# Starting every larger SBUF tile behind the first stage at a multiple of 128 bytes

## The chip, the cores and the metric

One core of one Trainium2 chip runs the whole kernel as one program. The metric is device time in microseconds (us): the median of three runs of the kernel before is 3519.21 us (3517.99 to 3523.26). One further execution was taken by the hardware profiler; all rows below are from it.

## The reference

Two transformer blocks of two layers each, on 1024 tokens of width 1024, in fp32. Cut to what matters here:

```
first_block, layers i = 0, 1:
    mix = diff_attention(h)  (i = 0)  or  pool_mixer(h)  (i = 1)
    h   = layer_norm(ALPHA * h + mix)          # mix ends in a 1024x1024 projection
    ffn = hier_moe(h)                          # 32 experts, 2 of them for each token
    h   = layer_norm(ALPHA * h + ffn)
hier_moe, for one expert:  y = (silu(x @ w_gate) * (x @ w_up)) @ w_down     # 1024 -> 512 -> 1024
second_block, layers l = 0, 1:
    h = rms_norm(x) * (1 + scale) + shift;  proj = h @ w_in
    x = x + gate * (concat(retention, mla, gla) @ w_out)
```

The result must have fp32 accuracy, so a product x @ w is computed as three products of rounded parts: high*high, high*low, low*high.

## The kernel before, in words

**Products.** `split` (L80, L81) makes the two fp32r parts of an operand: ScalarE writes the rounded copy, VectorE subtracts it from the original. `mm3` (L84 to L87) issues the three matmuls of one block of 128 rows. In `matmul(out, w, x)` the second argument is held in the array (stationary, 128x128, loaded by LDWEIGHTS), the third streams through it (moving, here mostly 512 columns).

**First stage** (0 to 303 us): `phase_qkv`, in the pools `pk0`, `v`, `p1` and `p1w`. Moving `xh`/`xl` or `wh`, stationary `whi`/`wlo` or `xh`/`xl`.

**Attention** (303 to 505 us): pools `p2k`, `p2c`, `p2p`; `oT` on the right side of SBUF.

**proj_ln** (twice, from 505 and from about 1390 us): for each of 8 tiles of 128 tokens, 16 `mm3` with stationary `ah`/`al` (parts of the activations; `first` for tile 0 of layer 0) and moving weights `wcut`, L87 and before; then layer norm and the router. Its pool is `pl`. In layer 1 two of the four weight pieces are in the pool `wo` on the right side, the other two in the pool `H`; a tile's 8 blocks of k use one piece of each for either half of the columns.

**Moe.run** (twice, from about 653 and from about 1540 us): for each of 32 experts 48 matmuls into `gu` (stationary `xgh`/`xgl`, the gathered tokens) and 24 into `accy` (stationary `hh`/`hl`), moving always `wcut`, plus 12 transposes. PE's order, ScalarE's and VectorE's are fixed by `in_order`. Each of the six pieces of weights of an expert (1 MB) is loaded by SyncE into a raw buffer `wraw` (nine of them in turn), split into one of four `wcut` buffers, and used by 12 matmuls. `gather` reads the tokens and `result` scatters the output by indirect DMA on GpSimd.

**Pooling.run** (1250 to 1390 us): stationary weights `wcut`, moving activations `x2` (the name `pool` in the trace): 64 `mm3` with 256 columns, then 96 with 512 columns; then the group products on `ph`.

**Second** (2110 us to the end): both layers of the second block, in `t4`, `rg`, `wr`, `mla`, `mle`, `ox`, `om`, `H`, `R` and others.

**Where tiles start.** Without a request the allocator rounds each tile's bytes per partition up to a multiple of 32 and puts one behind the other. A small tile therefore shifts all that come after it in its pool, and the pools stacked upon that one. Start addresses of the program before, as remainders of a division by 128 (first kernel stage, `H`, `R` and nearly all of `Second`: remainder 0):

| tile | role in the matmuls | remainder by 128 |
|---|---|---|
| `xgh`, `xgl`, `hh`, `hl` (MoE) | stationary | 64 |
| `ah`, `al` (proj_ln) | stationary | 64 |
| `x2` of Pooling (`pool` in the trace) | moving, 512 or 256 columns | 96 |
| `wcut` in the pool `wo` (proj_ln, layer 1) | moving, 512 columns | 96 |
| `wcut` in `H`, `first`, `xh`, `xl`, `whi`, `wlo`, `ph`, `mx` | stationary or moving | 0 |
| `p`, `pT`, `oraw`, `cmb`, `idb` (attention) | stationary or moving, 128 columns | 32 or 96 |
| `hT` (router) | stationary, 36 columns moving | 32 in layer 0, 0 in layer 1 |
| `wraw`, nine in turn in the MoE | not in a matmul | 0 (six), 96 (three) |

All tiles of remainder 0 that are used with 512 moving columns start 384 bytes beyond a multiple of 512. In the MoE the shift comes from the router's pool `rt`, below: its tiles `wr`, `br`, `lg`, `OH` and on take 15296 bytes, which is 64 more than a multiple of 128.

Of the kernel before, what the change touches and what calls it, by code (L numbers as in the profile page):

```python
# [17 lines left out]
PSUM = bass.MemoryType.PSUM  # L18
# [9 lines left out]
def host_consts():  # L28
    c = {}
    f = np.float32  # L30
    c["ident"] = np.eye(P, dtype=f)
    inv = (500000.0 ** (-np.arange(0, 16, 2) / 16)).astype(f)
    ang = (np.arange(S, dtype=f)[:, None] * inv[None, :]).astype(f)
    co, si = np.cos(ang).astype(f), np.sin(ang).astype(f)
    cT = np.tile(co.T, (8, 1))
    sT = np.concatenate([np.tile(si.T, (4, 1)), np.tile(-si.T, (4, 1))], 0)
    c["rope1"] = np.ascontiguousarray(np.stack([cT, sT], 1))
    i = np.arange(P)
    c["cmask"] = np.where(i[None, :] > i[:, None], f(-2.0 ** 100), f(0)).astype(f)
    c["iota"] = np.tile(np.arange(P, dtype=f)[None], (P, 1))  # L40

    kt = np.arange(2)[:, None, None] * np.array([0, S]) + np.arange(NT)[None, :, None] * P
    c["tcode"] = (kt[None] + i[:, None, None, None] - 2 * S).astype(f)
    c["tri"] = (i[:, None] < i[None, :]).astype(f)

    c["mavg"] = np.tile((1.0 / np.minimum(np.arange(1, 17)[None, :], np.array([2, 4, 8, 16])[:, None]))[None], (P, 1, 1)).astype(f)

    ch = i // 64
    lg = np.log1p(-np.exp2(-5.0 - np.arange(4)))
    vis = (ch[:, None] <= ch[None, :]).astype(np.float64)  # L50
    dm = np.exp(lg[None, :, None] * np.abs(i[:, None] - i[None, :])[:, None, :]) * vis[:, None, :] / 8.0
    c["r_dm"] = dm.astype(f)
    c["r_kw"] = (np.exp((127.0 - i)[:, None] * lg[None, :]) / 8.0).astype(f)
    hd = 2 * np.arange(2)[None, :] + ch[:, None]
    c["r_qw"] = np.exp((i + 1.0)[None, None, :] * lg[hd][:, :, None]).astype(f)
    c["r_sd"] = np.exp(128.0 * lg[hd]).astype(f)

    inv32 = (10000.0 ** (-np.arange(32) / 32)).astype(f)
    inv16 = (10000.0 ** (-np.arange(16) / 16)).astype(f)
    c["inv"] = np.stack([np.tile(inv32, 4), np.tile(inv16, 8)], 1).astype(f)  # L60
    c["rsgn"] = np.stack([np.tile(np.repeat([1.0, -1.0], 32), 2), np.tile(np.repeat([-1.0, 1.0], 16), 4)], 1).astype(f)
    c["bones"] = (ch[:, None] == ch[None, :]).astype(f)
    c["tri16"] = ((i[:, None] <= i[None, :]) & (ch[:, None] == ch[None, :])).astype(f) / f(16)
    same = ch[:, None] == ch[None, :]
    c["gmask"] = np.stack([(i[None, :] >= i[:, None]) & same, (i[None, :] < i[:, None]) & same], 1).astype(f)
    c["qmask"] = np.where(ch[None, :] > ch[:, None], f(-2.0 ** 100), f(0)).astype(f)
    return c


class Ctx:  # L70
    def __init__(self, tc, a):
        self.tc, self.nc, self.a = tc, tc.nc, a
        self.n = 0
# [192 lines left out]
class Attention:  # L266
# [50 lines left out]
    def tile(self):  # L317
        return self.PS.tile([P, S], F32, tag="S", name=self.g.name("S"), bufs=3)
# [1594 lines left out]
def b2_consts(g, pool, tmp):  # L1913
    nc, a = g.nc, g.a
    def load(name, shape):
# [21 lines left out]


CONST = host_consts()
INPUTS = ["x", "attn_w_qkv", "attn_w_o", "attn_lq1", "attn_lk1", "attn_lq2", "attn_lk2", "attn_sub_g", "pool_w_in",  # L1940
          "pool_w_grp", "pool_scale", "pool_w_out", "ln_g", "ln_b", "moe_w_grp_router", "moe_b_grp_router",
# [3 lines left out]


def program(tc, a, out):
    nc = tc.nc
    g = Ctx(tc, a)
    dram = lambda name, shape: nc.dram_tensor(name, shape, F32).ap()  # L1950
# [11 lines left out]
    with pool_of("const") as cp, ExitStack() as r2:  # L1962
# [106 lines left out]
        with ExitStack() as cb:  # L2069
            pool = cb.enter_context(L.pool("cb1", 3))  # L2070
# [51 lines left out]
```

## Time and profile before

| what | us |
|---|---|
| median of the three runs | 3519.21 |
| the profiled execution, its own time | 3515.97 |
| its span, first to last instruction | 3514.2 |
| TensorE busy in the span (PE) | 3299.4 |
| VectorE busy (DVE) | 2407.2 |
| ScalarE busy (ACT) | 1825.6 |

The profiled execution's time is 1.8 us above its span and 3.2 us below the median of the runs. A busy TensorE need not be one at its best rate: the end of a matmul is modelled, and matmuls overlap in the records (one lasts 388 to 394 ns, the next begins some 227 ns after it began). So its rate is read from the starts of consecutive matmuls, which a timeline gives to 10 ns, over long runs without a gap.

### The profile page before, as it was taken

What the parts mean: (1) busy time and instruction counts of PE and PEld (TensorE: products, weight loads), DVE (VectorE), ACT (ScalarE), POOL (GpSimd) and SP (SyncE); (2) the same over time, 40 slices, a digit from 0 to 9 for tenths busy, and PEclk for the clock granted to TensorE, in tenths of its full rate; (3) what the DMA queues carried; (4) which work ended last, traced back from release to release, by engine and by line L of the source; (5) the groups of instructions that cost most, each with busy time, mean ns of one, the idle gap of its engine ahead of it and who ended that gap; (6) DMA issues with size and microseconds to landing.
All of it is one profiled execution on the core that took longest, in us unless ns stands there. A gap on an engine that the chain in (4) does not pass through costs nothing. (4 is left out here: it accounts for less than half of the span.)

```text
span 3514.2 us, 44298 instructions
## 1 busy us (share of the span) xinstructions
PE 3299.4 (94%) x16904; PEld 2730.2 (78%) x16904; DVE 2407.2 (69%) x2850; ACT 1825.6 (52%) x2601; POOL 829.2 (24%) x627
## 2 busy tenths in 40 slices
PE   8999999999999969999999993999999899998988
PEld 7888878888888857888888882877777788676776
DVE  5665888799999975679999996532366443425653
ACT  3224872588878733248778772122467212244751
POOL 1121221133333231113333326321002122400120
PEclk9999999999999989999999996999999999999999
DMA  8666524699999832179999984211322632023144
GB/s 260 216 188 173 146 87 162 248 389 381 380 379 378 303 128 77 75 265 381 388 387 382 376 314 170 37 31 38 116 73 91 203 91 43 19 81 108 61 138 156
DMA packets 302967, 695.86 MB, mean 198 GB/s; under 512 B 57518, under 2 KB 154576, under 8 KB 286300
## 3 DMA queue, kind: packets, MB, share of 16 engines
q1 hardware_dynamic: 263964, 634.11, 51.8%
q0 software_dynamic: 36480, 50.45, 4.3%
q10 hardware_dynamic: 2304, 8.39, 0.6%
q8 instruction: 136, 2.23, 0.3%
q14 instruction: 83, 0.68, 0.1%
HBM read 625.59 MB, written 98.66 MB: 206 GB/s over the span
## 5 line engine op out<-in xcount | busy, mean ns | idle before, releaser
L81 DVE TENSOR_TENSOR wcut<-wraw,wcut 128x2048 fp32r<-128x2048 f32 (+1 forms) x401 | 902.7, 2267 | 66.7 <-ACT wcut L80 66.7
L80 ACT ACTIVATE wcut<-wraw 128x2048 fp32r<-128x2048 f32 (+1 forms) x401 | 754.0, 1900 | 124.8 <-PE accy L87 98.1
L85 PE MATMUL gu<-wcut,xgh 128*128 128x512 f32 x1024 | 408.7, 399 | 0.4 <-ACT xgh L80 0.4
L87 PE MATMUL gu<-wcut,xgl 128*128 128x512 f32 x1024 | 403.8, 394 | 0.0
L86 PE MATMUL gu<-wcut,xgh 128*128 128x512 f32 x1024 | 401.3, 392 | 0.0
L806 POOL DMA_INDIRECT yd<-yo,idx x64 | 171.4, 2679 | 799.8 <-DVE yo L805 780.2
L85 PE MATMUL A<-h,whi 128*128 128x512 f32 (+1 forms) x736 | 287.3, 391 | 6.2 <-ACT h L80 3.3
L87 PE MATMUL A<-h,wlo 128*128 128x512 f32 (+1 forms) x736 | 281.8, 383 | 3.8 <-DVE wlo L81 3.8
L86 PE MATMUL A<-h,whi 128*128 128x512 f32 (+1 forms) x736 | 282.8, 384 | 0.9 <-DVE h L81 0.9
L80 ACT ACTIVATE whi<-wraw 128x1024 fp32r<-128x1024 f32 (+2 forms) x86 | 70.9, 856 | 310.7 <-PE A L86 251.4
L85 PEld LDWEIGHTS gu<-wcut,xgh 128*128 128x128 f32 x1024 | 193.9, 189 | 38.4 <-ACT xgh L80 0.8
L86 PEld LDWEIGHTS gu<-wcut,xgh 128*128 128x128 f32 x1024 | 192.8, 188 | 39.3
L87 PEld LDWEIGHTS gu<-wcut,xgl 128*128 128x128 f32 x1024 | 192.4, 188 | 39.7 <-DVE xgl L81 0.9
L81 DVE TENSOR_TENSOR wlo<-wraw,whi 128x1024 fp32r<-128x1024 f32 (+2 forms) x86 | 83.1, 973 | 200.8 <-ACT whi L80 200.5
L87 PE MATMUL accy<-wcut,hl 128*128 128x512 f32 x512 | 201.9, 394 | 0.3 <-DVE hl L81 0.3
L86 PE MATMUL accy<-wcut,hh 128*128 128x512 f32 x512 | 200.6, 392 | 0.0
L85 PE MATMUL accy<-wcut,hh 128*128 128x512 f32 x512 | 199.1, 389 | 1.6 <-ACT hh L80 1.6
L746 POOL DMA_INDIRECT xg<-hd,idx x64 | 182.7, 2854 | 49.3 <-DVE idx L736 30.4
L85 PEld LDWEIGHTS A<-h,whi 128*128 128x128 f32 x736 | 144.8, 197 | 34.6 <-ACT h L80 4.5
L87 PEld LDWEIGHTS A<-h,wlo 128*128 128x128 f32 x736 | 143.8, 195 | 31.5 <-DVE wlo L81 4.7
L86 PEld LDWEIGHTS A<-h,whi 128*128 128x128 f32 x736 | 144.5, 196 | 27.6 <-issue 3.1
L1708 POOL TENSOR_TENSOR z<-z,lo 128x1024 f32<-128x1024 f32 x8 | 19.0, 2375 | 471.4 <-DMA lo<-rrd 235.8
(518 smaller groups left out, 7835.9 us busy)
## 6 DMA issues: line engine op xcount, KB each, us to landing
wraw<-in_moe_w_gate SPq DMA_DIRECT2D x128, 1024.0 KB
wraw<-in_moe_w_up SPq DMA_DIRECT2D x128, 1024.0 KB
wraw<-in_moe_w_down SPq DMA_DIRECT2D x128, 1024.0 KB
spare<-in_ada_w SPq DMA_DIRECT2D x48, 512.0 KB
wraw<-in_w_in SPq DMA_DIRECT2D x40, 512.0 KB
y<-yd SPq DMA_DIRECT2D x16, 1024.0 KB
wraw<-in_attn_w_qkv SPq DMA_DIRECT2D x12, 1024.0 KB
mx<-mixd SPq DMA_DIRECT2D x24, 512.0 KB
```

The lines of the kernel that those rows point to most:

```text
L80: self.nc.scalar.activation(hi, src, AF.Copy)
L81: (lo_eng or self.nc.vector).tensor_tensor(lo, src, hi.bitcast(F32), op=ALU.subtract)
L85: mm(out, wh, xh, start=start, stop=False)
L86: mm(out, wh, xl, start=False, stop=False)
L87: mm(out, wl, xh, start=False, stop=stop)
L746: self.g.nc.gpsimd.indirect_dma_start(out=xg, out_offset=None, in_=self.hd, in_offset=bass.IndirectOffsetOnAxis(ap=idx, axis=0), bounds_ch ...
L806: st = nc.gpsimd.indirect_dma_start(out=self.yd, out_offset=bass.IndirectOffsetOnAxis(ap=yidx, axis=0), in_=y, in_offset=None, bounds_chec ...
L1708: nc.gpsimd.tensor_tensor(z, z, rb, op=ALU.mult)
```

## The change

Two wrappers are put around the tile pools. Every tile whose elements per partition number 128 or more asks for a start at a multiple of 128 bytes, in all SBUF pools but the constants (`const`, and so `const2` too), `pk0`, `v` and those of the first stage (`p1`, `p1w`). Tiles of fewer elements are as before. No instruction is added or removed.

```diff
+class AlignedPool:
+    def __init__(self, pool):
+        self.pool = pool
+    def __getattr__(self, name):
+        return getattr(self.pool, name)
+    def tile(self, shape, dtype, **kw):
+        if math.prod(shape[1:]) >= 128:
+            kw["align_bytes"] = 128
+        return self.pool.tile(shape, dtype, **kw)
+
+class Aligned:
+    def __init__(self, tc):
+        self.tc = tc
+    def __getattr__(self, name):
+        return getattr(self.tc, name)
+    @contextmanager
+    def tile_pool(self, **kw):
+        with self.tc.tile_pool(**kw) as pool:
+            yield pool if kw.get("space") is PSUM or kw["name"].startswith(("const", "pk0", "v", "p1")) else AlignedPool(pool)
...
 def program(tc, a, out):
+    tc = Aligned(tc)
     nc = tc.nc
     g = Ctx(tc, a)
```

## Rows read from the trace of the kernel before

**Rows 1.** The page: TensorE's busy time, share and instructions

```profile
PE 3299.4 (94%) x16904; PEld 2730.2 (78%) x16904; DVE 2407.2 (69%) x2850; ACT 1825.6 (52%) x2601; POOL 829.2 (24%) x627
```

**Rows 2.** Busy time by stretch: proj_ln, MoE, Pooling, proj_ln, MoE; header names the columns

```profile
core 0: us, PE busy (x) PEld busy (x) DVE busy (x) ACT busy (x) POOL busy (x), PEclk, DMA share, GB/s
528.00:612.00 84.00, 84.00 (x444) 70.87 (x443) 70.69 (x185) 25.01 (x40) 11.35 (x10) 1.00 0.43 157
660.00:1130.00 470.00, 469.62 (x2204) 392.00 (x2203) 446.48 (x314) 377.43 (x316) 147.94 (x50) 1.00 0.99 378
1300.00:1350.00 50.00, 50.00 (x216) 40.32 (x216) 36.95 (x45) 13.03 (x17) 16.57 (x17) 1.00 0.07 22
1400.00:1500.00 100.00, 98.75 (x520) 82.90 (x519) 59.48 (x119) 18.95 (x29) 13.95 (x11) 1.00 0.24 91
1560.00:2060.00 500.00, 500.00 (x2347) 417.67 (x2346) 478.00 (x335) 400.91 (x337) 162.96 (x56) 1.00 1.00 381
```

**Rows 3.** Waits, 700 to 1100 us: total us, times, longest; releaser behind the arrow

```profile
ACT wcut L80 <- PE accy L87: 37.6, 46, 0.8
DVE wcut L81 <- ACT wcut L80: 17.7, 22, 0.8
```

**Rows 4.** Waits of SyncE's queue, which issues the loads, 700 to 1100 us

```profile
SPq L121 <- DVE wcut L81: 343.1, 135, 3.3
```

**Rows 5.** Busy time in two gapless runs of matmuls: first stage, then MoE

```profile
92.75:112.24 19.49, 19.49 (x87) 16.14 (x86) 13.31 (x21) 3.05 (x5) 0.57 (x1) 1.00 0.50 162
909.43:922.47 13.04, 13.04 (x58) 10.71 (x57) 12.23 (x9) 11.42 (x9) 2.37 (x1) 1.00 1.00 362
```

**Rows 6.** Timeline, proj_ln layer 0: start us, us, instruction; 9, then 33 matmuls between

```profile
526.63 0.39 PE L85 MATMUL acc<-wcut,first 128*128 128x512 f32 x1
...
528.67 0.39 PE L85 MATMUL acc<-wcut,ah 128*128 128x512 f32 x1
...
536.22 0.39 PE L85 MATMUL acc<-wcut,ah 128*128 128x512 f32 x1
```

**Rows 7.** Timeline, Pooling, 512 columns: 45 matmuls from the first to the second

```profile
1300.97 0.40 PE L85 MATMUL acc<-pool,wcut 128*128 128x512 f32 x1
...
1311.47 0.40 PE L85 MATMUL acc<-pool,wcut 128*128 128x512 f32 x1
```

**Rows 8.** Timeline, proj_ln layer 1: 9, then 11 matmuls between

```profile
1409.02 0.40 PE L85 MATMUL acc<-wcut,ah 128*128 128x512 f32 x1
...
1411.13 0.39 PE L85 MATMUL acc<-wcut,ah 128*128 128x512 f32 x1
...
1413.65 0.39 PE L87 MATMUL acc<-wcut,al 128*128 128x512 f32 x1
```

**Rows 9.** Timelines, 256 columns: first stage (33 matmuls between), Pooling (30 between)

```profile
67.92 0.28 PE L85 MATMUL acc<-whi,xh 128*128 128x256 f32 x1
...
71.89 0.28 PE L85 MATMUL acc<-whi,xh 128*128 128x256 f32 x1
...
1280.83 0.28 PE L85 MATMUL acc<-pool,wcut 128*128 128x256 f32 x1
...
1284.43 0.28 PE L85 MATMUL acc<-pool,wcut 128*128 128x256 f32 x1
```

**Rows 10.** Groups by shape: count, busy us, mean ns, idle before; first of three lines

```profile
L85 PE MATMUL gu<-wcut,xgh 128*128 128x512 f32 x1024 | 408.7, 399 | 0.4 <-ACT xgh L80 0.4
L87 PE MATMUL accy<-wcut,hl 128*128 128x512 f32 x512 | 201.9, 394 | 0.3 <-DVE hl L81 0.3
L85 PE MATMUL acc<-wcut,ah 128*128 128x512 f32 x240 | 96.7, 403 | 0.0
L85 PE MATMUL acc<-pool,wcut 128*128 128x512 f32 x96 | 38.1, 397 | 0.0
```

**Rows 11.** Tile wcut, 700 to 1100 us: duration ns min/median/max, first and last start

```profile
L80 ACT ACTIVATE wcut<-wraw x135: 1912/1918/1927, 699.9 to 1099.7; 128x2048 fp32r<-128x2048 f32 x135
L81 DVE TENSOR_TENSOR wcut<-wraw,wcut x135: 2280/2289/2295, 700.2 to 1098.7; 128x2048 fp32r<-128x2048 f32 x135
```

## The prediction

> **What bounds the kernel now.** I read the page first: TensorE is busy for 94% of the span [rows 1]. [...] Next the waits, to see who paces whom in the MoE. The reader is to see three things. No row has TensorE waiting. ScalarE waits for TensorE to give back a buffer of split weights (37.6 us in 400), and VectorE waits behind ScalarE (17.7 us) [rows 3]. And each of the 135 weight loads of that stretch waits until VectorE has emptied a raw buffer [rows 4], so the loads run behind the matmuls and not ahead of them, though the queues are busy for 0.99 of the time [rows 2]. TensorE sets the pace there, and whatever each matmul saves should come out at the end.
>
> Last I read the starts of consecutive matmuls, the one thing that an address could change. These are the pairs of rows to compare. In the first stage, with all operands at remainder 0, 87 matmuls start within 19.49 us; from first to last start (92.75 to 112.25) that is 86 steps in 19.50 us, 226.7 ns each. In the MoE, with a stationary operand at remainder 64, 57 steps take 13.05 us (909.43 to 922.48), 228.9 ns each [rows 5]. Heavier loading could make the same difference, so I looked for a place where nothing changes but the address. In proj_ln of layer 0 the stationary tile changes from `first` (0) to `ah`/`al` (64) in the middle of a run, with the moving weights in the same pool: 9 steps take 2.04 us (226.7 ns) up to that point and 33 steps take 7.55 us (228.8 ns) behind it [rows 6]. The step is there at the very matmul where the tile changes.
>
> **The change part by part.** It adds and removes no instruction; it moves tiles by 32 to 96 bytes. What can change is the rate of instructions that touch them, and the address overlaps from which the program takes its waits.
>
> Stationary tiles from 64 to 0, moving operand at 0. The MoE has (1024 + 512) x 3 = 4608 such matmuls over both layers [rows 10]. At 228.9 - 226.7 = 2.2 ns that is 10.1 us. proj_ln has 240 x 3 = 720 with `ah`/`al` [rows 10]; 192 of them, in layer 1, stream weights from the pool `wo` and are counted below. The other 528 give 528 x 2.2 = 1.2 us.
>
> Moving tiles from 96 to 0. In Pooling, 45 steps of 512 columns take 10.50 us, 233.3 ns [rows 7]; 96 x 3 = 288 matmuls [rows 10] at 233.3 - 226.7 = 6.6 ns give 1.9 us. In proj_ln of layer 1 both operands are off: 9 steps take 2.11 us (234.4 ns) with weights from `wo`, and the next 11, weights from `H`, take 2.52 us (229.1 ns) with the same stationary tile [rows 8]. From 234.4 to 226.7 ns, 192 matmuls give 1.5 us.
>
> Moves that I cost at nothing. Pooling's 192 matmuls of 256 columns have a moving operand at 96 and take 3.60 us for 30 steps, 120.0 ns; those of the first stage, all at 0, take 3.97 us for 33, 120.3 ns [rows 9]. At that width the address does not show, and I take it that it shows no more at 128 columns (attention, transposes, router), where the work per load is smaller still; if it did, as much as 2.2 ns on some 1500 such matmuls of the attention would be 3 us. On ScalarE and VectorE, the weights' splits read raw buffers at 0 and at 96 in turn, and all 135 lie between 1912 and 1927 ns and between 2280 and 2295 ns [rows 11]; I take 0 there. The DMAs into those raw buffers are hidden as long as the loads wait for buffers and not the reverse [rows 4]. If a load became late, its cover would be gone and ScalarE's split and then TensorE would stand; I bound this as a rival. Waits from overlaps: tiles move by less than 128 bytes while the tiles they may touch are 2 to 16 KB long, so I expect the same pairs to overlap; the bound is a wait or two of the length seen in the stage, 0.8 us [rows 3].
>
> The sum is 10.1 + 1.2 + 1.9 + 1.5 = 14.7 us. How much of it reaches the end? In the MoE all, by the reading above: afterwards an expert's 72 matmuls take 0.16 us less, and VectorE, with 446.48 us of 470 [rows 2], the next in line, is free for 0.9 us in each of the 26 or so experts of that stretch. In proj_ln and Pooling, 4.6 us, nearly all; I keep 0 to 4.6 for the range. The profiled execution would go from 3515.97 to 3501.3 us. Its time stood 3.2 us below the median of the runs; carried over, the median goes from 3519.2 to 3504.5 us. I say 3504.
>
> [...]
>
> **The rivals.**
>
> *No change: the starts are not what makes the difference* (5%). If every 32-byte start were alike, the steps in rows 6 and 8 would need another cause. What could be one is the second tile that `ah` and `al` are, against the single `first`; but the first stage uses two tiles as well, `whi` and `wlo`, and runs at 226.7 ns. The time would be 3519. That the change doesn't reach its tiles is part of this rival; the pools concerned are none of the names left out.
>
> *The MoE keeps its pace, something else taking over* (9%). VectorE is at 95% there and the queues at 0.99 with 378 GB/s [rows 2]. If a split or load came last instead, the MoE's 10.1 us would be lost and the other 4.6 us would stay: 3514.6 us, within 0.2%. Against it: the waits all point from TensorE outward [rows 3, 4], and the demand grows by only 1%.
>
> *Slower: the remainder that counts is not that of 128* (5%). Every tile shown fast starts 384 bytes beyond a multiple of 512; none shows another multiple of 128. Adding up `rt`'s tiles with the request, `xgh` and `ah` will start at a multiple of 512 itself. Should that phase be a bad one for a stationary operand, the worst step in the rows is 234.4 ns [rows 8]: the 5136 matmuls that now take 228.9 would pay 5.5 ns more, 28.2 us, less the 1.9 us of Pooling, whose tiles move down by 96 bytes to the proven phase: 3519.2 + 26.3 = 3545.5 us. It decides from a step of about 229.3 ns on, where the loss takes up Pooling's gain.
>
> *A better phase still* (4%). By the same gap in the evidence the new place could be faster than 226.7 ns. Nothing in the rows bounds that; at a second 2.2 ns it is another 11 us: 3493.
>
> **How the numbers follow.** The forecast holds 77%. A measurement of this kernel can tell about 0.2%, 7 us, from no change; faster means below 3512.2 us, which is half of the sum, so some loss on the way still counts as faster. Forecast and better phase give 0.81 faster, the two rivals without effect 0.14 same, the bad phase 0.05 slower. For the range: the forecast's own bounds are the 4.6 us outside the MoE lost (3509) and runs that lie 1 to 4 us from their median, as before's do. [...] Downward I go to 3496, upward to 3514, which takes in most of a partial loss in the MoE.
>
> **What would show it.** In the changed kernel's trace, runs of 512-column matmuls in the MoE step by 226.7 ns, and the durations of their three lines, 388, 392 and 394 ns, become one value near 389. Rows 6 lose the step at `ah`; Pooling and `wo` step by 226.7 as well. TensorE's busy time falls by about 14 us with the same 16904 matmuls; the second block from 2110 us on is only shifted. I am wrong if the step in the MoE stays at 228.9 or above, or if it falls and TensorE then has waits for VectorE or ScalarE in the MoE, or if idle time between the stages grows by what the matmuls save.

## The result and the profile after

| | kernel before | changed kernel |
|---|---|---|
| median, us (four runs of each) | 3519.08 | 3554.78 |
| lowest and highest, us | 3517.99, 3523.26 | 3552.24, 3558.52 |
| span of the profiled execution, us | 3514.2 | 3552.0 |

The changed kernel is slower: 35.7 us, a ratio of 1.0100 with a 95% interval of 1.0084 to 1.0116. The page's row of the engines, which answers [rows 1], has the same 16904 matmuls busy for 21.9 us more:

```profile
PE 3321.3 (94%) x16904; PEld 2726.5 (77%) x16904; DVE 2414.0 (68%) x2850; ACT 1827.7 (51%) x2601; POOL 712.4 (20%) x627
```

**Where it came from.** TensorE's order is nearly the same in both, so the same matmul can be looked up in both timelines (start us, duration us, engine, line, tiles, shape, in brackets the idle time before it and what ended it). First the kernel before: first matmul of Pooling, of the second block, of its two output stages, and the last of all.

```profile
1259.53 0.80 PE L85 MATMUL acc<-pool,wcut 128*128 128x256 f32 x2 [0.49 <-ACT pool L80]
...
2154.62 0.80 PE L85 MATMUL A<-h,whi 128*128 128x256 f32 x2 [1.11 <-ACT h L80]
...
2742.53 0.80 PE L85 MATMUL acc<-r,mx 128*128 128x512 f32 x1 [5.36 <-DMA mx<-mixd]
...
3408.03 0.80 PE L85 MATMUL acc<-r,mx 128*128 128x512 f32 x1 [5.28 <-DMA mx<-mixd]
...
3504.01 0.39 PE L87 MATMUL acc<-r,mx 128*128 128x512 f32 x1
```

The same five in the changed kernel (its lines are 30 higher):

```profile
1268.24 0.58 PE L115 MATMUL acc<-pool,wcut 128*128 128x256 f32 x1 [0.49 <-ACT pool L110]
...
2167.24 0.79 PE L115 MATMUL A<-h,whi 128*128 128x256 f32 x2 [1.11 <-ACT h L110]
...
2764.46 0.79 PE L115 MATMUL acc<-r,mx 128*128 128x512 f32 x1 [14.63 <-DMA mx<-mixd]
...
3445.35 0.80 PE L115 MATMUL acc<-r,mx 128*128 128x512 f32 x1 [14.64 <-DMA mx<-mixd]
...
3541.82 0.39 PE L117 MATMUL acc<-r,mx 128*128 128x512 f32 x1
```

The reader is to see three losses and one gain. Before Pooling the changed kernel is 8.7 us late, the first MoE. At the second block it is 12.6 us late: Pooling and proj_ln of layer 1 gave some back, the second MoE took as much as the first. And each output stage now begins behind a gap of 14.6 us on TensorE where 5.3 to 5.4 us stood.

**The matmuls are slower, not idle.** The same 58 matmuls of the MoE that took 13.04 us in [rows 5] (columns as in [rows 2]) take 13.27; from their first start to their last, 57 steps, that is 232.9 ns each instead of 228.9:

```profile
913.29:926.56 13.27, 13.27 (x58) 10.72 (x57) 12.30 (x9) 11.48 (x9) 0.16 (x1) 1.00 1.01 372
```

In [rows 6] `first` stepped by 226.7 ns and slowed down where `ah` came. Now `first` is slow as well: 13 steps to the second line below take 3.02 us, 232.3 ns. And in the second block, where [rows 2] and the prediction had nothing to say, the products with `h` step by 233.4 ns (29 steps in 6.77 us):

```profile
525.02 0.39 PE L116 MATMUL acc<-wcut,first 128*128 128x512 f32 x1
...
528.04 0.40 PE L117 MATMUL acc<-wcut,first 128*128 128x512 f32 x1
...
2239.21 0.39 PE L115 MATMUL A<-h,whi 128*128 128x512 f32 x1
...
2245.98 0.40 PE L117 MATMUL A<-h,wlo 128*128 128x512 f32 x1
```

**The gap ahead of the output stage.** SyncE's queue at that point (start us, duration us, line, transfer, count). In the kernel before, six loads of `mx` go out before the stores of the last attention result (`mixd<-tb`, `mixd<-lo`):

```profile
2738.08 3.89 SPq L1834 DMA_DIRECT2D mx<-mixd  x6
2746.30 0.33 SPq L1309 DMA_DIRECT2D mixd<-tb  x1
2747.56 0.33 SPq L1310 DMA_DIRECT2D mixd<-lo  x1
```

In the changed kernel all twelve stand behind them:

```profile
2756.29 1.23 DVE L1336 TENSOR_TENSOR z<-u,z 128x1024 f32<-128x1024 f32 x1 [2.23 <-POOL z L1738]
2758.63 0.34 SPq L1339 DMA_DIRECT2D mixd<-tb  x1
2759.89 0.33 SPq L1340 DMA_DIRECT2D mixd<-lo  x1
2760.26 6.88 SPq L1864 DMA_DIRECT2D mx<-mixd  x12
```

The addresses say why. An aligned tile does not only start at a multiple of 128: the pool sets 128 bytes more aside for each of its tags. So `R`'s tiles stand 128 to 768 bytes higher and `u1` in the pool `mla` 1536 higher (186240 to 187776), while `mx`, on the right, stands 256 or 128 lower (190336 to 190080 or 190208). Before, `u1` ended at 190336, the byte at which `mx` began. Now it reaches into it by 1664 to 1792 bytes, and the loads have to wait for the multiplication that reads `u1` last (`z<-u,z` above); in the queue they now stand behind the stores that come after it.

### The profile page after: what moved, and what is told of

It reads as the page before. It is cut to its first block, busy times and chain, and to the rows that moved or that the text cites. A ratio compares the mean times of both kernels' runs of the same rounds, so it can differ in the third digit from the quotient of the medians.

```text
span 3552.0 us, 44293 instructions
## 1 busy us (share of the span) xinstructions
PE 3321.3 (94%) x16904; PEld 2726.5 (77%) x16904; DVE 2414.0 (68%) x2850; ACT 1827.7 (51%) x2601; POOL 712.4 (20%) x627
## 5 line engine op out<-in xcount | busy, mean ns | idle before, releaser
L115 PE MATMUL acc<-r,mx 128*128 128x512 f32 x256 | 104.8, 410 | 34.7 <-DMA mx<-mixd 29.3
L110 ACT ACTIVATE xgh<-tp 128x512 fp32r<-128x512 f32 x128 | 76.2, 597 | 82.9 <-PE tp L128 82.9
```

The lines of the kernel that those rows point to most:

```text
L110: self.nc.scalar.activation(hi, src, AF.Copy)
L115: mm(out, wh, xh, start=start, stop=False)
```

## The experiments

### g1_grid: the price of the starts by itself

```diff
+ for m, ml, s, sl in grid():        # bytes beyond a multiple of 512: moving hi, lo, stationary hi, lo
+     for k in range(8):
+         xh, xl = at(MOVING + m + 2048 * k, 512), at(MOVING_LO + ml + 2048 * k, 512)
+         wh, wl = at(STILL + s + 512 * k, P), at(STILL_LO + sl + 512 * k, P)
+         mm(acc, wh, xh), mm(acc, wh, xl), mm(acc, wl, xh)     # start and stop left out here
```

> The price of the addresses by itself. The kernel computes nothing of the reference: it splits no weights and runs no layer, it loads x into SBUF and issues 510 groups of 24 matmuls (8 times the three of mm3, 512 moving columns, fp32r, 128x128 stationary), each group with the start of the moving parts and of the stationary parts at chosen distances from a multiple of 512 bytes; nothing else uses SBUF meanwhile. Read: the step between starts inside a group. Theory 1 (remainder by 512, and only the relation of the two operands): 226.7 ns wherever moving and stationary have the same remainder, in steps of 32 bytes, whatever it is; about 232 to 233 ns where they differ as in the MoE of the changed kernel (moving 384, stationary 0), 228.9 at (384, 320), 233.4 at (480, 384). Theory 2 (384 itself is the good place): 226.7 only where both are 384, the other equal pairs (0, 0), (128, 128), (256, 256) above 229. Theory 3 (that of the prediction, remainder by 128): 226.7 in all pairs made of 0, 128, 256 and 384. Theory 4 (addresses do nothing, the other engines' traffic does): 226.7 in all groups.

The kernel has 525 groups, not the 510 of the expectation. In 256 of them both parts of an operand start alike: all 16 x 16 pairs of starts, in steps of 32 bytes. They were read from the starts of the fourth to the 22nd matmul of each group; the very first group, whose first ten steps took 300 to 590 ns, is left out. Only one thing separates them: the distance of the moving from the stationary start, as a remainder by 256.

| moving less stationary start, by 256 | 0 | 32 | 64 | 96 | 128 | 160 | 192 | 224 |
|---|---|---|---|---|---|---|---|---|
| step, ns, median of 32 pairs (31 for 0) | 227.2 | 233.2 | 228.9 | 233.9 | 233.3 | 234.6 | 233.3 | 233.3 |
| lowest | 226.7 | 233.0 | 228.9 | 233.3 | 232.7 | 234.3 | 233.3 | 233.0 |
| highest | 227.8 | 233.4 | 228.9 | 233.9 | 233.4 | 234.6 | 233.3 | 233.3 |

Five of the groups in the timeline, two starts of each with 14 matmuls between them: moving and stationary remainder by 512 at (384, 384), (128, 384), (384, 320), (480, 384) and (384, 0).

```profile
1166.95 0.39 PE L52 MATMUL acc<-buf 128*128 128x512 f32 x1
...
1170.35 0.39 PE L52 MATMUL acc<-buf 128*128 128x512 f32 x1
...
1122.35 0.39 PE L52 MATMUL acc<-buf 128*128 128x512 f32 x1
...
1125.75 0.39 PE L52 MATMUL acc<-buf 128*128 128x512 f32 x1
...
988.43 0.39 PE L52 MATMUL acc<-buf 128*128 128x512 f32 x1
...
991.87 0.39 PE L52 MATMUL acc<-buf 128*128 128x512 f32 x1
...
1183.55 0.39 PE L52 MATMUL acc<-buf 128*128 128x512 f32 x1
...
1187.05 0.39 PE L52 MATMUL acc<-buf 128*128 128x512 f32 x1
...
96.52 0.40 PE L52 MATMUL acc<-buf 128*128 128x512 f32 x1
...
100.02 0.39 PE L52 MATMUL acc<-buf 128*128 128x512 f32 x1
```

3.40 us, 3.40, 3.44, 3.50 and 3.50 us for 15 steps: 226.7, 226.7, 229, 233 and 233 ns. The second pair settles it against theory 1 as it was put (a remainder by 512): 128 and 384 differ by 256 and are as fast as equal ones. Theories 2 and 3 fall too: 384 is no special place, and pairs of multiples of 128 take 226.7 or 233.3 ns. From 10 us on VectorE and GpSimd were busy for 0.00 us, ScalarE for 17.1 of 2890 us, at a DMA share of 0.00, so theory 4 falls as well. Another 512 to 7680 bytes on top of distance 0 changed nothing (226.7 ns).

In 240 further groups the high and the low part of an operand start at different multiples of 128. In 192 of them distances 0 and 128 are mixed within `mm3`. These step by 228.5 to 233.3 ns, by the pattern: 233.2 ns in the mean where the high stationary part is at 128 from both moving parts and the low one at 0, 231.5 ns where it is the reverse. The table is thus for parts at equal distances; which of the pairs within a mixed pattern sets the step was not worked out.

With this table every row of the kernel before reads anew: the MoE's 228.9 ns in [rows 5] is distance 64 (384 less 320), Pooling's 233.3 in [rows 7] distance 96 (480 less 384), the 234.4 with `wo` in [rows 8] distance 160 (480 less 320), the fast rows distance 0. The changed kernel's MoE has `wcut` at 384 and `xgh` at 0: distance 128 (so has `xgl`, and `hh` at 256; `hl` alone, at 384, has distance 0). Its products with `h` are of the mixed pattern at 233.2 ns, `whi` at 128 and `wlo` at 0.

### e2_moe0: the new remainder of the MoE and proj_ln alone

```diff
-        with near("rt", 1) as rt:
+        with near("rt", 1) as rt, near("pad", 1) as pad:
+            pad.tile([P, 48], F32, name=g.name("pad"))        # the same in layer 1
```

> The kernel before with one empty tile of 192 bytes above the router's tiles in both layers, nothing else: xgh, xgl, hh, hl, ah, al go from remainder 320 (by 512) to 0, which is also 0 by 128. If the remainder by 512 counts, with the steps of the changed kernel (232.6 against 228.9 ns, 5136 matmuls): 19 us more, 3538 us. If that of 128 counts: 4608 + 528 matmuls x 2.2 ns less, 3508. If the MoE of the changed kernel is slower through something else, its moved raw buffers or its queues: 3508 to 3519.

3534.29 us beside 3519.33 (ratio 1.0045, 1.0030 to 1.0061): 15.0 us slower, with all queues, buffers and the order of every engine as before. The 58 matmuls again:

```profile
913.90:927.14 13.24, 13.24 (x58) 10.74 (x57) 12.32 (x9) 11.48 (x9) 0.17 (x1) 1.00 1.00 371
```

The remainder of 128 is 0 here and the MoE is slower, so it isn't the one that counts. The expectation of 19 us had taken the worst run of steps; over whole experts a matmul became 3.1 ns slower, not 3.7, and 5136 x 3.1 ns is 16 us.

### e3_mla512 and e7_mla512b: the overlap alone

```diff
+            late.tile([P, 128], F32, name=self.g.name("pad"))
             self.mla(late, early)
```

> The kernel before with one empty tile of 512 bytes at the bottom of the pool mla, in both layers of the second block, so that u1 (which ended at 190336, the very byte at which mx starts) reaches 512 bytes into the first mx buffer, as it does in the changed kernel; all remainders by 512 stay as they were. If that overlap holds the loads of mx back behind the last products of the attention, each output stage begins some 10 us later: 3539 us. If the gap there comes from slower loads or from the addresses of the operands: 3519.

3539.78 us beside 3519.33, 20.5 us slower (ratio 1.0057, 1.0041 to 1.0072). SyncE's queue has turned as in the changed kernel:

```profile
2744.84 0.34 SPq L1309 DMA_DIRECT2D mixd<-tb  x1
2746.10 0.33 SPq L1310 DMA_DIRECT2D mixd<-lo  x1
2746.47 6.87 SPq L1834 DMA_DIRECT2D mx<-mixd  x12
```

and TensorE waits as long, by the waits from 2735 to 2780 us (engine and line, releaser, total us, times, longest):

```profile
PE acc L85 <- DMA mx<-mixd: 17.6, 2, 14.8
```

So 512 bytes of overlap between `u1` and `mx` cost some 10 us in each of the two layers, with no matmul's step changed. e7 is the same kernel once more, next to e6 below:

> e3_mla512 once more, beside e6_left128 on the same chip, to have the difference between the two from runs side by side: 3539.8 as before. e6 less this is the price of the second block's slower steps alone: 17.7 us by theory 1, about 8 by theory 2, 0 by theory 3.

It gave 3538.37 us beside 3519.14, 19.2 us slower.

### e4_first: without the second block

```diff
-            yield pool if ... kw["name"].startswith(("const", "pk0", "v", "p1")) else AlignedPool(pool)
+            yield pool if ... kw["name"].startswith(("const", "pk0", "v", "p1", "H_", "R_", "tmp2")) else AlignedPool(pool)
...
     def pool(self, name, bufs, **kw):          # of Second
-        return self.g.tc.tile_pool(...)
+        return self.g.tc.tc.tile_pool(...)
```

> The changed kernel without its second block: H, R and all pools of Second stay as in the kernel before, the pools of the first block are aligned to 128. So mx no longer overlaps u1 and all matmuls of the second block have equal remainders again. If e3's 20 us and the second block's slower steps (about 1500 matmuls at 233.3 instead of 226.7 ns, some at 230) are what the second block lost, this gives 3554.8 less 20 to 33. Worked out from g1's steps for the remainders that this program has by 256 (moving 128; xgh 128 with xgl 0, or both 0 apart by 128; hh and hl likewise): MoE 3072 x 2.4 + 1536 x 3.4 ns, proj_ln 1.3 us, Pooling and wo 2.2 us less: 3531 us. If the remainder by 128 counted: 3504. If the second block's losses came from the first (a later start, other queues): near 3555.

3525.75 us beside 3518.46 (ratio 1.0018, 1.0009 to 1.0028): 29 us less than the changed kernel, with 7.3 us of loss left in the first block. That is 5 us less than worked out; the MoE's steps were those expected (231.3 ns in the median for `gu`, g1's 231.5), and the interval reaches to 9.9 us. Because `R` is lower here, `xgh` and `xgl` have other remainders than in the changed kernel (distances 0 and 128 mixed), and the first block is faster too: in the profiles the second block begins at 2163.72 instead of 2167.24 us. So some 25 of the 29 us are the second block's, which is also what the timelines above give it (37.8 less 12.6 us).

### e6_left128: the second block's steps

```diff
+        r2.enter_context(near("hp", 1)).tile([P, 32], F32, name=g.name("pad"))
         H, R = r2.enter_context(near("H", 4)), r2.enter_context(near("R", 1))
```

> The kernel before with one empty tile of 128 bytes below the pool H, so that all pools of the left side behind the attention move up by 128 bytes and those of the right side stay. In the first block the relation of moving and stationary stays (MoE and proj_ln: 64, Pooling: 224 instead of 96, both 233.3 ns). In the second block the weights whi/wlo and mx, on the right, now differ by 128 from h and the weights r, on the left: 1920 + 768 matmuls at 233.3 instead of 226.7 ns, 17.7 us; and u1 reaches 128 bytes into mx, as in e3 (+20.5). Theory 1 (both costs reach the end): 3519 + 38 = 3557. Theory 2 (in the second block slower steps are made up elsewhere, by a clock that falls less between the products, as 9.4 us in the two profiles suggest): about 3547. Theory 3 (TensorE's steps do not set the pace there): 3540, as e3.

3542.96 us beside 3519.14 (ratio 1.0066, 1.0053 to 1.0079), and e7 on the same chip 3538.37: 4.6 us more for 2688 matmuls whose steps did become slower (three took 695 ns in the median for `h` with `whi`, 696 for `r` with `mx`, 680 before), 5 to 5.5 ns each, some 14 us in all. The runs of e6 lie between 3540.3 and 3544.3 us and those of e7 between 3534.4 and 3546.4, so the 4.6 us are not clear of zero. But the far ends of the two intervals, 1.0079 and 1.0048, are only 11 us apart: theory 1, with its 17.7 us, falls.

The profiles show where a part of it went. First e7 (columns as in [rows 2]): the stretch from the first matmul of the second block to its first output stage, that output stage up to the next layer, and the same two of the second layer.

```profile
2155.04:2753.95 598.91, 542.93 (x2805) 438.70 (x2805) 299.50 (x401) 259.50 (x480) 140.76 (x138) 0.94 0.24 71
2753.95:2858.59 104.64, 98.11 (x440) 80.32 (x440) 41.12 (x40) 18.46 (x25) 21.51 (x14) 0.96 0.64 202
2858.59:3428.04 569.45, 529.80 (x2764) 427.34 (x2765) 268.38 (x364) 242.89 (x461) 110.65 (x119) 0.96 0.23 66
3428.04:3523.66 95.62, 91.75 (x383) 74.61 (x384) 26.97 (x28) 8.06 (x14) 4.69 (x7) 0.95 0.57 175
```

Then e6:

```profile
2154.92:2752.87 597.95, 541.43 (x2805) 434.58 (x2805) 299.59 (x401) 259.12 (x480) 140.59 (x138) 0.95 0.24 71
2752.87:2860.11 107.24, 100.76 (x441) 80.97 (x441) 41.12 (x40) 18.47 (x25) 21.46 (x14) 0.95 0.62 197
2860.11:3433.09 572.98, 531.13 (x2765) 427.00 (x2765) 268.53 (x364) 242.62 (x461) 110.41 (x119) 0.96 0.23 65
3433.09:3532.18 99.09, 95.04 (x383) 75.65 (x384) 26.97 (x28) 8.05 (x14) 4.69 (x7) 0.94 0.54 169
```

And e3, which is the kernel of e7:

```profile
2153.64:2750.80 597.16, 538.72 (x2805) 435.31 (x2805) 299.56 (x401) 259.33 (x480) 140.82 (x138) 0.95 0.25 71
2750.80:2856.15 105.35, 98.84 (x441) 80.69 (x441) 41.12 (x40) 18.47 (x25) 21.54 (x14) 0.95 0.63 200
2856.15:3433.93 577.78, 536.10 (x2764) 432.68 (x2765) 268.51 (x364) 242.86 (x461) 110.56 (x119) 0.95 0.23 65
3433.93:3529.81 95.88, 91.94 (x384) 74.75 (x384) 26.96 (x28) 8.05 (x14) 4.69 (x7) 0.95 0.57 174
```

An output stage has 384 matmuls `r` with `mx`, whose slower steps sum to 2.1 us. It takes 1.9 to 2.6 us longer in e6 in layer 0 and 3.2 to 3.5 us in layer 1. There the steps reach the end, and theory 3 does not hold. In the stretches ahead, with the 1920 matmuls with `h`, e6 is 1.0 us faster than e7 in layer 0 and 3.5 us slower in layer 1; but e3 is 1.8 us faster than e7 and 8.3 us slower, and it is the same kernel. So what these matmuls cost at the end is not shown.

Nor is theory 2, that the clock makes it up. The mean granted clock of the first stretch is 0.94 in e7 and 0.95 in e6, but 0.95 in e3 too. The 9.4 us of the expectation came from four places (2318, 2438, 2888 and 3103 us of the kernel before) where the granted clock of the kernel before is 0.50 for 3.4 to 6.8 us (at the first of them the starts of nine steps, from 2320.55 to 2324.39 us, lie 427 ns apart) and that of the changed kernel for less (3.5 us) or not at all (1.00), its lag shrinking by 1.8, 3.1, 1.4 and 3.1 us. Such falls come and go without slower steps: over 40 us around the third place the granted clock is 0.96 in the kernel before (2862 to 2902 us) and 1.00 in e2 (2877.5 to 2917.5 us), where the second block's tiles start as before.

### e1_pad384 and e5_pad256: the distance made 0

```diff
+            pad.tile([P, 16], F32, ...)        # 64 bytes above rt and rt1: xgh, xgl, hh, hl, ah, al
+            with near("hp", 1, side="right") as hp, near("hT", 1, side="right") as tp:
+                hp.tile([P, 24], F32, ...)     # 96 bytes: Pooling's x2 (in e1 inside hT, without effect)
+            w1.enter_context(near("wp", 1, side="right")).tile([P, 24], F32, ...)     # 96 bytes: wo
```

> The kernel before with four empty tiles and nothing else: 64 bytes above the router's tiles in both layers, 96 bytes below Pooling's x2 and below the weights in wo. So xgh, xgl, hh, hl, ah, al, x2 and the weights in wo start 384 bytes behind a multiple of 512, as all tiles do that were fast in the kernel before. If the remainder by 512 counts, the sum of the prediction comes out here: 4608 + 528 matmuls x 2.2 ns, 288 x 6.6, 192 x 7.7: 14.7 us less, 3504.4 us. If the MoE's steps fall and its time does not (VectorE or the loads take over): 3514.6. If the starts do nothing: 3519.

3510.01 us beside 3519.33 (ratio 0.9981, 0.9968 to 0.9993): 9.3 us faster, not 14.7. In e1 `x2` stayed at its old start, so 1.9 us were still to come:

> e1_pad384 with the empty tile for Pooling in a pool of its own, so that x2 now does move down by 96 bytes (in e1 the allocator had put the empty tile below and left x2 where it was). All matmuls of 512 columns in the first block then have equal remainders by 256. Pooling's 288 matmuls go from 233.3 to 226.7 ns, 1.9 us less than e1: about 3508 us. If what e1 lacked against its 14.7 us came from something other than the steps behind the transposes, it stays at 3510.

e5 took 3508.63 us beside 3518.46, 9.8 us faster (ratio 0.9974, 0.9965 to 0.9984), and has the lowest median here. The half microsecond by which it gained more than e1 lies inside both intervals, so Pooling's 1.9 us show in its steps and not in the time. Pooling now steps by 226.9 ns, in its timeline (44 steps from the first to the second line, one to the third: 10.21 us for 45, where [rows 7] had 10.50):

```profile
1295.86 0.39 PE L87 MATMUL acc<-pool,wcut 128*128 128x512 f32 x1
...
1305.85 0.39 PE L86 MATMUL acc<-pool,wcut 128*128 128x512 f32 x1
1306.07 0.39 PE L87 MATMUL acc<-pool,wcut 128*128 128x512 f32 x1
```

and the 58 matmuls of the MoE take 12.96 us:

```profile
907.75:920.71 12.96, 12.96 (x58) 10.71 (x57) 12.16 (x8) 11.37 (x9) 2.39 (x1) 1.00 1.02 370
```

The rest of the missing gain is in the MoE, behind the transposes. In e1 the eleven steps from the first line below, the second matmul behind four transposes, to the second line take 2.54 us, some 230.5 ns each; the 21 from there to the third take 4.76 us, 226.7 ns:

```profile
800.64 0.39 PE L86 MATMUL gu<-wcut,xgh 128*128 128x512 f32 x1
...
803.18 0.39 PE L85 MATMUL accy<-wcut,hh 128*128 128x512 f32 x1
...
807.94 0.39 PE L85 MATMUL accy<-wcut,hh 128*128 128x512 f32 x1
```

Over 22 experts this slow stretch costs 40 ns each time, in the same pattern (229, 233, 236, 224, 231, 236, 228, 233, 231 ns). Two of them in each of 64 experts are 5.2 us. 14.7 less 5.2 is 9.5 us; e5 gained 9.8, by its interval 5.6 to 12.3, so 14.7 lies outside.

### g2_turns: the slow stretch by itself

```diff
+ for k in range(4):
+     nc.tensor.transpose(tp[:, k], src[:, k // 2, k % 2], ids[:, 136 * i:136 * i + P])
+ ...                                  # then 24 matmuls as in g1, at distance d
```

> Again the price by itself; nothing of the reference is computed. Groups of 4 (also 0 or 8) fp32 transposes as in the MoE (moving ident, stationary a view of every second element), then 24 matmuls as mm3 issues them. In e1_pad384 the 10 matmuls behind each group of transposes took 229, 233, 236, 224, 231, 236, 228, 233, 230 and 227 ns instead of 226.7 though moving and stationary had equal remainders by 256, and with a distance of 64 (the kernel before) there was no such stretch. Theory A (the transposes' own operands set it): among the 64 pairs of starts of ident and of the transposed tile some have no slow stretch at distance 0. Theory B (any interruption by transposes does it, wherever their operands are): all 64 pairs show it, some 30 to 40 ns for each group, and the groups without transposes don't. Theory C (the traffic of the other engines does it): no group here shows it, 226.7 from the second matmul on.

Theory C falls: the stretch is there with no other engine at work. So does B as it was put: it is not the same for all. Of the 63 pairs that ran at full clock at distance 0 (the mean of the whole run is 0.996), the cost over 21 steps goes from 8 ns (two slow steps, 233 and 230 ns) to 48, median 28; a group without transposes that follows another distance has it too (235, 229, 232, 231, then 227). At distance 64 it is 9 ns in the median, at most 13. Where `ident` and the transposed tile start as in the MoE (both 128 by 256), 41 ns: the sum of 229, 234, 236, 224, 231, 235, 229, 232 and 231 above 226.7. So the transposes' starts set how long it lasts (theory A in part: none of the pairs is free of it). Moving `ident` or `xg` for this was not tried: `xg` shares its tiles with operands whose distance is already 0.

## Why the prediction was wrong, point by point

**TensorE sets the pace in the MoE.** Right. e2 made its steps slower and the kernel 15.0 us slower, e5 made them faster and gained what the steps gave; no split or load took over: the two MoE stretches became 2.1 us shorter each in e5's profile, beside the 4.8 us in all that their steps gave (227.9 instead of 228.9 ns in the mean, over 4608). The rival that something else takes over is not seen in any run.

**The step that failed first: "Stationary tiles from 64 to 0", that the remainder by 128 is what counts.** The rows had shown three slow remainders and one fast, but always against the same other operand: every fast tile started at 384 by 512, and so did every partner, but for `wo`, where both were off. From that one can't tell a remainder from a distance. g1 shows a distance, by 256. By it the change made the MoE and proj_ln slower where the sum had a gain of 10.1 and 1.2 us: distance 128 instead of 64, and 15.0 us lost (e2). The sum itself was nearly sound for the right address: with distance 0 the same 5136 + 480 matmuls gain 9.8 us (e5). What it lacked there is the slow stretch behind the transposes, 5.2 us.

**The rival "the remainder that counts is not that of 128".** This came nearest, at the right place, though as a bad phase of the stationary start and not as a distance (in g1 a stationary start at 0 is fast wherever the moving one is at 0 or 256): the prediction had worked out that `xgh` would start at a multiple of 512, had put the doubt about the phase into words, and gave it 5%. Its price was 5.5 ns for each of 5136 matmuls, 28.2 us; measured were 3.1 ns and 15.0 us. That its 3545.5 us stand nearest to the measured 3554.8 is in part luck: the overlap, which it did not have, fills the place of what its price had too much. The chance was too low: four places in the rows agreed with the favoured rule, but they were not four tests of it.

**The step that failed second: "it moves tiles by 32 to 96 bytes", so "I expect the same pairs to overlap".** `R`'s last tile moved by 768 bytes, `u1` by 1536, and a new pair overlaps. The bound of a wait or two of 0.8 us came from waits in the MoE [rows 3] and not from the place where left and right side of SBUF meet; the cost there is 10 us a layer (e3, e7: 20.5 and 19.2 us). What the prediction should have priced is not the wait of one instruction but the loss of a head start: the first output products, which began at 2742.53 us in the kernel before, ahead of the last stores at 2746.30 and 2747.56, were cover for the tail of the attention.

**"The second block from 2110 us on is only shifted."** Failed too. All its tiles already started at multiples of 128, but they moved against each other: `whi` and `wlo` to distances 128 and 0 from `h`, `R`'s tiles each by another amount from `mx`. e6 puts the price of such a shift at 4.6 us, which is not clear of the runs' spread; in the output stages it shows at 2 to 3.5 us each.

**Pooling and `wo`.** For Pooling direction and size were right: its 288 matmuls of 512 columns take 70.79 instead of 72.45 us from first to last start, 1.7 us less where the sum had 1.9, although one of `x2`'s four tiles has a distance of 128 from its partner. For `wo` the term failed: `wcut` and `ah` moved from distance 160 to 128, by g1's table 1.3 ns a step and not 7.7. From Pooling's first matmul to the second block's first the loss grew by 3.9 us while the second MoE alone took 8.8, so Pooling and proj_ln gave back some 4.9. Only part of that is steps; the rest is within what two profiles differ by (e3, which leaves the first block as it was, is 1.4 us faster in Pooling).

**The sum as it came out.** 12.6 us in the first block by the trace, 19.2 to 20.5 from the overlap, 4.6 from the second block's steps: 36 to 38 us, beside the 35.7 measured. The first two parts are shown by experiments of their own; the third is what e6 and e7 differ by, and its size is open.

**The range, 3496 to 3514 us.** Its lower end lies 4 us below what 3504 and the most that runs of the kernel before lie from their median, 4 us, give; no run shows a term for these further 4 us, which were the author's estimate. What the runs showed is that a granted clock of 0.50 comes and goes: at the four places named under e6 it stands for 3.4 to 6.8 us in the profile of the kernel before, and at one of the four, for 3.5 us, in that of the changed kernel.

## What to carry to other kernels

For fp32r matmuls of 512 columns, look at the start of the moving tile less that of the stationary tile, as a remainder by 256, before any alignment of single tiles; here 0 is best, and empty tiles of 64 and 96 bytes gained 9.8 us where the alignment of all tiles lost 35.7. A request for alignment also takes room: compare the addresses of the whole program and look for new overlaps where two stacks of pools meet. When all examples of a rule share one partner, an experiment that moves the partner belongs ahead of the rule.

## What the runs showed of the hardware

- The step of an fp32r matmul of 512 columns with a 128x128 stationary operand goes from 226.7 to 234.6 ns with the distance of the two operands' starts by 256, in steps of 32 bytes; a shift of both by the same amount, or by 256 and more on top, changes nothing (g1). Where the high and low parts have different distances, 0 and 128, it is 228.5 to 233.3 ns by the pattern.
- At distance 0 the fast step is not there at once: behind transposes 2 to 8 of the next nine steps are slow, 8 to 48 ns in all, depending on where the transposes' operands start (g2); at distance 64 the 228.9 ns are there nearly at once. So the second best distance gives up less than the table says when transposes come every 24 matmuls: some 40 of the 53 ns that 24 steps would gain are lost again.
- Slower steps need not cost their sum: in the second block some 14 us of slower steps cost 4.6 us by the medians and less than 11 by the intervals (e6, e7). In the output stages they cost about their sum or more; where the rest went is open, as two profiles of one kernel differ by up to 8.3 us in a stretch of some 570 us (e3, e7).
